# Gate matmuls that write a PSUM bank in order, and an evacuation that reads it with a stride

## The chip, the cores and the metric

One Trainium2 chip, one core of it. Times are device microseconds (us) of one execution of the whole program. Three runs of the kernel before gave 2480.03, 2481.56 and 2482.59 us; the median, 2481.56 us, is the number that the changed kernel is compared with. TensorE is written PE, VectorE DVE, ScalarE ACT, GpSimd POOL, and SyncE, which issues the transfers here, SP.

## What is computed

Two transformer blocks over 512 tokens of width 1024. The change lies in the last part, the feed-forward part of the second block (PEER): every token picks, in each of 8 heads, 16 of 128 x 128 = 16384 experts, and its output is a gated sum over them.

```
top, pos = lax.top_k(cand, PEER_TOPK)
eidx = jnp.take_along_axis(cidx, pos, axis=-1)
g = jax.nn.softmax(top, axis=-1)
u = u_tab[eidx]
v = v_tab[eidx]
a = jax.nn.gelu(jnp.einsum('thkd,td->thk', u, ht))
out = jnp.einsum('thk,thkd->td', g * a, v)
```

## The kernel before

For 384 of the 512 tokens (`ND`) the kernel does not gather expert rows. It computes all 16384 scores of a token densely, and multiplies them by a dense matrix of gates that is zero where a token did not pick an expert. (The other 128 tokens are gathered row by row, by POOL's indirect transfers, later.) An expert number is 128 * ia + ib. `peer_gates` (from L1528) builds the gates, for three tiles of 128 tokens in turn, each in four chunks of 32 tokens (`GC`), each chunk in two groups of 16 tokens (`GN`): 24 groups in all.

For a group DVE writes four tensors of 128 x 2048 fp16: `gob`, one-hot in ib (L1553); `goa`, one-hot in ia (L1554); `goh`, which is `goa` times the upper half of the gate (L1555); and `goa` again, times the lower half (L1556). Each of the three names has two buffers. For each token PE then multiplies `gob` with `goh` and with `goa`, and both products add up in PSUM (L1561): a matrix of 128 (ib, on the partitions) by 128 (ia), which is this token's gates. Four tokens share one PSUM bank of 512 fp32, so a group has 32 matmuls, each with its own weight load, and 4 banks. ACT reads each bank and writes it, scaled, to `gst` (L1563), whose layout is ib x ia x 32 tokens; after 8 banks a chunk is full and SP writes its 2 MB to HBM (L1566, tensor `gates`, 12 writes). `gst` has two buffers, the PSUM pool of `gg` six.

Between the groups the kernel also works ahead on the scores: `ahead` (called at L1565) loads 512 KB of one table (`uTr`), splits it into two fp16 halves (`uTh` on ACT, L121; `uTl` on DVE, L122), multiplies them by the tokens (`pu`, 24 matmuls of 128 x 384, L141) and applies GELU on ACT (`pa`, L1589). A scheduler sets the order on PE, DVE and ACT in this part, and each engine works through its own list in order. On PE the first product of each of a group's four banks (`goh`, 4 matmuls) stands ahead of the other 28.

Behind this part the main loop of the PEER block begins: for each of 128 ia it reads the gates back (`pg`, L1602), multiplies them with the scores on POOL (`pag`, L1605), splits the result (`pw`, L121 and L122) and multiplies it with the second table (`pacc`, L1614).

Of the kernel before, what the change touches and what calls it, by code (L numbers as in the profile page):

```python
# [14 lines left out]
AF = mybir.ActivationFunctionType  # L15
# [4 lines left out]
P = 128  # L20
# [17 lines left out]
GS = 10  # L38
# [16 lines left out]
class Block:  # L55
# [1410 lines left out]
    def pairs(self, vp, qp, val, idx, eng):  # L1466

        nc = self.nc
        eng.tensor_scalar(idx[0], idx[0], 128.0, None, op0=OP.mult)
        cand = vp.tile([P, 4, 50], F32, name="cand", tag="cand", bufs=2)  # L1470
        cidx = vp.tile([P, 4, 50], F32, name="cidx", tag="cidx", bufs=2)
        for to, dst, (a, b) in ((nc.vector, cand, val), (eng, cidx, idx)):
            off = 0
            for i, ni, j, nj in PAIRS:
                n = ni * nj
                d = dst[:, :, off:off + n].rearrange("p t (i j) -> p t i j", i=ni)
                to.tensor_tensor(d, b[:, :, None, j:j + nj].to_broadcast([P, 4, ni, nj]),
                                  a[:, :, i:i + ni, None].to_broadcast([P, 4, ni, nj]), op=OP.add)
                off += n
        return cand, cidx  # L1480
# [47 lines left out]
    def peer_gates(self, wk, e, g, gd, tt, ahead):  # L1528

        nc = self.nc  # L1530
        f = wk.tile([P, 2, P], F32, name="gab", tag="gab", bufs=1)
        nc.vector.tensor_scalar(f[:, 0], e, 1.0 / 128, -63.5 / 128, op0=OP.mult, op1=OP.add)
        nc.vector.tensor_scalar(f[:, 0], f[:, 0], 1.5 * 2.0 ** 23, -1.5 * 2.0 ** 23, op0=OP.add, op1=OP.add)
        nc.vector.scalar_tensor_tensor(f[:, 1], f[:, 0], -128.0, e, op0=OP.mult, op1=OP.add)
        ps = self.ps1("gtp")
        for j, x in enumerate((f[:, 0], f[:, 1], g)):
            nc.tensor.transpose(ps[:, P * j:P * (j + 1)], x, self.ident)

        twice = lambda x: x.unsqueeze(len(x.shape)).to_broadcast([*x.shape, 2])
        idx = wk.tile([P, 2, P, 2], F16, name="gidx", tag="gidx", bufs=2)  # L1540
        gs = wk.tile([P, 2, P, 2], F16, name="gsp", tag="gsp", bufs=2)
        nc.scalar.activation(idx, twice(ps[:, :2 * P].rearrange("p (j t) -> p j t", j=2)), AF.Copy)
        gp = twice(ps[:, 2 * P:3 * P])
        nc.scalar.activation(gs[:, 0], gp, AF.Copy, scale=2.0 ** GS)
        nc.vector.scalar_tensor_tensor(gs[:, 1], gp, 2.0 ** GS, gs[:, 0], op0=OP.mult, op1=OP.subtract)
        pairs = lambda x: x.rearrange("p t (i j) -> p t i j", j=2)
        iota = pairs(self.iota128[:, None, :]).to_broadcast([P, GN, P // 2, 2])
        for c in range(P // GC):
            stage = wk.tile([P, P, GC], F32, name="gst", tag="gst", bufs=2)
            for n in range(c * GC, c * GC + GC, GN):  # L1550
                col = lambda t: t[:, n:n + GN, None, :].to_broadcast([P, GN, P // 2, 2])
                b, a, hi = (wk.tile([P, GN, P], F16, name=f"go{x}", tag=f"go{x}", bufs=2) for x in "bah")
                nc.vector.tensor_tensor(pairs(b), iota, col(idx[:, 1]), op=OP.is_equal)  # L1553
                nc.vector.tensor_tensor(pairs(a), iota, col(idx[:, 0]), op=OP.is_equal)  # L1554
                nc.vector.tensor_tensor(pairs(hi), pairs(a), col(gs[:, 0]), op=OP.mult)  # L1555
                nc.vector.tensor_tensor(pairs(a), pairs(a), col(gs[:, 1]), op=OP.mult)  # L1556
                for q in range(0, GN, 4):
                    ps = self.ps1("gg").rearrange("p (i t) -> p i t", t=4)
                    for t in range(4):
                        for j, x in enumerate((hi, a)):  # L1560
                            nc.tensor.matmul(ps[:, :, t], b[:, q + t], x[:, q + t], start=j == 0, stop=j == 1)  # L1561
                    o = n - c * GC + q
                    nc.scalar.activation(stage[:, :, o:o + 4], ps, AF.Copy, scale=2.0 ** -GS)  # L1563
                if (n == c * GC or c % 2) and len(ahead.a) < LAG - REST:
                    ahead(early=False)  # L1565
            nc.sync.dma_start(gd[:, tt * (P // GC) + c], stage)  # L1566
# [326 lines left out]
```

## Time and profile before

| | |
|---|---|
| median of 3 runs | 2481.56 us (2480.03 to 2482.59) |
| the profiled execution, its time | 2484.21 us |
| its span, from the first to the last instruction | 2482.5 us |
| what lies around the span | 1.7 us |
| PE busy in the span | 2355.9 us (95%) |
| DVE busy | 1771.0 us (71%) |
| ACT busy | 932.2 us (38%) |
| gate matmuls, first to last start | 1419.7 to 1582.5 us |
| first matmul of the main loop's sum `pacc` | 1599.5 us |

All times in the rows below are counted from the start of the span. A matmul's duration in a row reaches from its start to the end of its way through the array, and the next one starts before that; so the pace of a run of matmuls is read from their starts, or from the pieces of the chain of waits, which give a length and a count. The granted clock is a share of 2.4 GHz: 1.00 is 2.4 GHz, 0.5 is 1.2 GHz.

### The profile page before, as it was taken

Reading aid. Unit: us, or ns where it says so; the run is one execution under the profiler, and the core shown is the slowest. Engines: PE = TensorE matmul, PEld = TensorE weight load, DVE = VectorE, ACT = ScalarE, POOL = GpSimd, SP = SyncE. Lnnn points to the kernel's source line nnn. Section 1 sums busy time; section 2 is a strip of 40 time slices with the busy share of each in tenths; the row PEclk is TensorE's granted clock in tenths of the full one; section 3 lists DMA queues with packets and bytes.
Section 4 is the critical chain, followed back from the end, with each engine's and each line's share of the span. In section 5 each row is a group of like instructions: output and inputs, shape, how many; then the busy total and the mean of one; then the engine's idle time right before and its main releaser. Section 6 shows DMA issues by size and latency. Waiting matters only on the chain.

```text
span 2482.5 us, 35960 instructions
## 1 busy us (share of the span) xinstructions
PE 2355.9 (95%) x13424; PEld 1199.5 (48%) x13424; DVE 1771.0 (71%) x3285; ACT 932.2 (38%) x1593; POOL 760.7 (31%) x757
## 2 busy tenths in 40 slices
PE   6998999989999999899899799999999999999998
PEld 3444444444443343355354477655555555555443
DVE  5998658653333332568489977688888888999896
ACT  4554543231111111365356654443333333333333
POOL 2124000000000000001157500146666666666773
PEclk9998999989999999999999999999999999999999
DMA  3411139979999998222242155659999999999895
GB/s 132 131 44 44 37 141 324 334 284 417 419 419 414 401 399 347 87 69 69 103 133 70 60 200 216 221 194 354 335 338 332 337 338 329 333 342 333 294 331 175
DMA packets 186322, 613.16 MB, mean 247 GB/s; under 512 B 17971, under 2 KB 71772, under 8 KB 159900
## 3 DMA queue, kind: packets, MB, share of 16 engines
q1 hardware_dynamic: 148988, 476.44, 52.2%
q0 software_dynamic: 36864, 134.23, 14.7%
q8 instruction: 107, 1.75, 0.3%
q14 instruction: 75, 0.61, 0.1%
q10 hardware_dynamic: 288, 0.11, 0.0%
HBM read 579.58 MB, written 27.28 MB: 244 GB/s over the span
## 4 chain that ended last, share of the span: by engine, by line
PE 62%; DVE 9%; issue 3%; ACT 3%; DMA 1%; POOL 0%; SPq 0%; DVEq 0%; ACTq 0%; POOLq 0%
PE pacc L1614 17%; PE pu L141 17%; PE w L764 9%; PE py L806 5%; PE pj L141 3%; PE gg L1561 3%; PE comb L757 2%; PE disp L731 2%; PE wout L141 2%; DMA vNr<-in_vN_dram 1%; PE pq L141 1%; DVE pef L1517 1%; DVE wlo L122 1%; DVE gacc L1771 1%; DVE t L1626 1%
## 5 line engine op out<-in xcount | busy, mean ns | idle before, releaser
L141 PE MATMUL pu<-pn,uTh 128*128 128x384 f16 x2048 | 502.8, 328 | 7.6 <-ACT pa L1589 5.7
L1614 PE MATMUL pacc<-vNh,pw 128*128 128x512 f16 x1536 | 474.2, 380 | 5.7 <-DVE pw L122 4.3
L1614 PEld LDWEIGHTS <-pw 128*128 128x128 f16 x2304 | 224.5, 98 | 275.1 <-DVE pw L122 13.1
L141 PE MATMUL pu<-pn,uTl 128*128 128x384 f16 x1024 | 335.9, 328 | 5.5 <-POOL uTl L1577 4.8
L1614 PE MATMUL pacc<-vNl,pw 128*128 128x512 f16 x768 | 292.2, 380 | 2.5 <-DVE vNl L122 2.5
L141 PEld LDWEIGHTS <-uTh 128*128 128x128 f16 x2048 | 202.1, 99 | 148.1 <-ACT uTh L121 5.8
L121 ACT ACTIVATE vNh<-vNr 128x1024 f16<-128x1024 f32 x128 | 135.2, 1056 | 315.5 <-PE pacc L1614 286.7
L764 PE MATMUL w<-wx,xt 128*64 128x512 f32 x1024 | 253.0, 597 | 0.0
L141 PEld LDWEIGHTS <-whi 128*128 128x128 f16 x1744 | 159.7, 99 | 180.9 <-issue 24.6
L1742 POOL DMA_INDIRECT row<-in_pu_dram,pe x128 | 198.7, 1552 | 125.4 <-DVE row L1764 102.5
L1742 POOL DMA_INDIRECT row<-in_pv_dram,pe x128 | 197.0, 1539 | 122.7 <-DVE gacc L1771 93.6
L122 DVE SCALAR_TENSOR_TENSOR vNl<-vNr,vNh 128x1024 f16<-128x1024 f32 x128 | 169.1, 1321 | 91.2 <-ACT vNh L121 91.1
L1142 POOL MEMSET cvu<- 128x2 f32 x4 | 0.4, 96 | 755.9 <-PE w L764 755.9
L1605 POOL TENSOR_TENSOR pag<-pa,pg 128x384 f32<-128x384 f32 x128 | 152.0, 1188 | 200.8 <-DMA pg<-gates 184.3
L122 DVE SCALAR_TENSOR_TENSOR uTl<-uTr,uTh 128x1024 f16<-128x1024 f32 x113 | 175.1, 1549 | 28.7 <-ACT uTh L121 23.2
L141 PE MATMUL pj<-wx,whi 128*128 128x512 f16 x624 | 189.3, 384 | 2.0 <-ACT wx L121 1.8
L1771 DVE SCALAR_TENSOR_TENSOR gacc<-row,ga,gacc 128x1024 f32<-128x1024 f32 x127 | 184.1, 1450 | 2.2
L1764 DVE SCALAR_TENSOR_TENSOR row<-row,htok 128x1024 f32<-128x1024 f32 x128 | 178.1, 1436 | 0.0
L122 DVE SCALAR_TENSOR_TENSOR wlo<-wraw,whi 128x1024 f16<-128x1024 f32 x97 | 130.0, 1341 | 47.7 <-ACT whi L121 47.3
L758 DVE SCALAR_TENSOR_TENSOR hT<-comb,hT 128x512 f32<-128x512 f32 x128 | 80.5, 684 | 110.9 <-PE comb L757 110.8
L1589 ACT ACTIVATE pa<-pu 128x384 f32<-128x384 f32 x128 | 62.2, 486 | 226.6 <-PE pu L141 226.5
L764 PEld LDWEIGHTS w<-wx,xt 128*64 128x64 f32 x1024 | 74.5, 137 | 141.1 <-issue 138.1
(456 smaller groups left out, 3900.3 us busy)
## 6 DMA issues: line engine op xcount, KB each, us to landing
wx<-in_w_dram SPq DMA_DIRECT2D x192, 1024.0 KB
uTr<-in_uT_dram SPq DMA_DIRECT2D x128, 512.0 KB
vNr<-in_vN_dram SPq DMA_DIRECT2D x128, 512.0 KB
wraw<-in_win_dram SPq DMA_DIRECT2D x57, 512.0 KB
wada<-in_wada_dram SPq DMA_DIRECT2D x48, 512.0 KB
gates<-gst SPq DMA_DIRECT2D x12, 2048.0 KB
pg<-gates SPq DMA_DIRECT2D x32, 768.0 KB
wraw<-in_wq_dram SPq DMA_DIRECT2D x16, 512.0 KB
```

The costliest lines, as they stand in the source:

```text
L121: self.nc.scalar.activation(hi, src, AF.Copy, scale=scale)
L122: self.nc.vector.scalar_tensor_tensor(lo, src, scale, hi, op0=OP.mult, op1=OP.subtract)
L141: self.nc.tensor.matmul(ps, w[a][:, ks[k], :], act[b][:, k, cols], start=first and k == only[0] and j == 0, stop=last and k == only[-1] an ...
L758: nc.vector.scalar_tensor_tensor(hT[:, m], ps, 2.0 ** -AS, hT[:, m], op0=OP.mult, op1=OP.add)
L764: nc.tensor.matmul(ps[64 * b:64 * b + 64], xt[q][:, 4 * c + k, 64 * b:64 * b + 64], w[b][:, k], start=c == 0 and k == 0, stop=c == 1 and k ...
L806: nc.tensor.matmul(py[d][64 * b:64 * b + 64], ht[:, f, 64 * b:64 * b + 64], w[b][:, f], start=f == 0, stop=f == 3)
L1561: nc.tensor.matmul(ps[:, :, t], b[:, q + t], x[:, q + t], start=j == 0, stop=j == 1)
L1605: nc.gpsimd.tensor_tensor(c3(ag), c3(a), self.gt[:, :, ia % 4, :], op=OP.mult)
L1614: self.nc.tensor.matmul(acc[2 * t + c], w[x][:, P * t:P * (t + 1)], v[y][:, 512 * c:512 * c + 512], start=ia == 0 and j == 0, stop=ia == P ...
L1742: nc.gpsimd.indirect_dma_start(out=t, out_offset=None, in_=I[table], in_offset=bass.IndirectOffsetOnAxis(ap=self.e[:, s:s + 1], axis=0))
L1764: nc.vector.scalar_tensor_tensor(x, x, 1.0, self.ht, op0=OP.mult, op1=OP.mult, accum_out=self.a[:, s:s + 1])
L1771: nc.vector.scalar_tensor_tensor(self.acc, x, self.a[:, s:s + 1], self.acc, op0=OP.mult, op1=OP.add)
```

## The change

The gate matmul of token t in its bank wrote its 128 fp32 results in steps of four elements (16 bytes), token innermost: PSUM held ia x 4 tokens. Now it writes 128 elements in a row, and PSUM holds 4 tokens x ia. ACT's copy, which used to read the bank from front to back, now reads for each ia four elements that are 128 elements (512 bytes) apart. What it writes is as before: for each ia a run of four tokens (16 bytes) in `gst`, the runs 128 bytes apart.

```
         for q in range(0, GN, 4):
-            ps = self.ps1("gg").rearrange("p (i t) -> p i t", t=4)
+            ps = self.ps1("gg")
             for t in range(4):
                 for j, x in enumerate((hi, a)):
-                    nc.tensor.matmul(ps[:, :, t], b[:, q + t], x[:, q + t], start=j == 0, stop=j == 1)
+                    nc.tensor.matmul(ps[:, P * t:P * (t + 1)], b[:, q + t], x[:, q + t], start=j == 0, stop=j == 1)
             o = n - c * GC + q
-            nc.scalar.activation(stage[:, :, o:o + 4], ps, AF.Copy, scale=2.0 ** -GS)
+            nc.scalar.activation(stage[:, :, o:o + 4], ps.rearrange("p (t i) -> p i t", t=4), AF.Copy, scale=2.0 ** -GS)
```

No instruction is added, removed or moved: the list of each of the five engines, and of every transfer, is the same row for row. Only the two access patterns in PSUM differ.

## Rows read from the trace of the kernel before

**Rows 1.** Busy time by stretch: us, PE, PEld, DVE, ACT, POOL busy, granted clock, DMA share, GB/s.
```profile
1440.00:1460.00 20.00, 20.00 (x155) 15.92 (x153) 16.75 (x16) 10.41 (x17) 0.00 (x0) 1.00 0.61 221
...
1419.70:1582.60 162.90, 151.80 (x1164) 121.66 (x1164) 127.91 (x118) 82.61 (x134) 0.00 (x0) 1.00 0.53 200
...
1600.00:2200.00 600.00, 600.00 (x3238) 316.32 (x3237) 526.40 (x639) 228.92 (x316) 378.01 (x283) 1.00 0.89 319
```

**Rows 2.** Waits of DVE, 1419.7 to 1582.6: us in total, times, longest.
```profile
DVE gob L1553 <- PE gg L1561: 19.4, 9, 2.4
DVE uTl L122 <- ACT uTh L121: 7.0, 1, 7.0
DVE uTl L122 <- PE pu L141: 5.5, 1, 5.5
```

**Rows 3.** Chain of waits, gate matmuls of two groups in a row: start us, us, what.
```profile
1479.56 3.52 PE gg L1561 x32
...
1484.38 3.07 PE gg L1561 x28
```

**Rows 4.** Line L1561: duration ns min/median/max, first and last start.
```profile
L1561 PE MATMUL gg<-goa,gob x384: 269/315/315, 1422.0 to 1582.6; 128*128 128x128 f16 x192
```

**Rows 5.** Line L731, the dispatch of the first block, same columns.
```profile
L731 PE MATMUL disp<-disp,ut x1024: 218/220/315, 529.4 to 984.9; 128*128 128x128 f16 x171
```

**Rows 6.** Timeline of PE in the dispatch: start us, us, engine, line, what, count.
```profile
536.38 1.96 PE L731 MATMUL disp<-disp,ut 128*128 128x128 f16 x32
```

**Rows 7.** Busy time by stretch, two stretches of the dispatch.
```profile
529.30:532.80 3.50, 3.43 (x34) 3.18 (x34) 3.33 (x6) 0.74 (x3) 0.00 (x0) 0.54 0.84 269
536.30:538.30 2.00, 2.00 (x36) 1.82 (x34) 0.35 (x1) 0.73 (x2) 0.00 (x0) 1.00 0.49 82
```

**Rows 8.** Timeline of DVE in the gates' part, six of its instructions.
```profile
1463.18 1.21 DVE L1556 TENSOR_TENSOR goa<-goa,gsp 128x2048 f16<-128x2048 f16 x1
...
1464.54 0.29 DVE L1526 TENSOR_TENSOR pgate<-pgate,pgs 128x128 f32<-128x128 f32 x1
...
1481.56 1.22 DVE L1556 TENSOR_TENSOR goa<-goa,gsp 128x2048 f16<-128x2048 f16 x1
...
1483.83 1.22 DVE L1554 TENSOR_TENSOR goa<-iota,gidx 128x2048 f16<-128x2048 f16 x1
...
1519.44 1.22 DVE L1556 TENSOR_TENSOR goa<-goa,gsp 128x2048 f16<-128x2048 f16 x1
...
1577.20 1.22 DVE L1556 TENSOR_TENSOR goa<-goa,gsp 128x2048 f16<-128x2048 f16 x1
```

**Rows 9.** Chain of waits, the last 28 matmuls of two later groups.
```profile
1522.32 3.06 PE gg L1561 x28
...
1579.86 3.06 PE gg L1561 x28
```

**Rows 10.** Timeline behind the last group: SP's write of the gates, DVE's split.
```profile
1583.58 0.33 SPq L1566 DMA_DIRECT2D gates<-gst  x1
...
1598.47 0.78 DVE L122 SCALAR_TENSOR_TENSOR pw<-pag,pw 128x384 f16<-128x384 f32 x1 [1.46 <-ACT pw L121]
```

**Rows 11.** Groups on ACT, 1419.7 to 1582.6: busy us, mean ns; idle before, releaser.
```profile
L1563 ACT ACTIVATE gst<-gg 128x512 f32<-128x512 f32 x95 | 56.7, 597 | 49.3 <-PE gg L1561 38.7 <-issue 9.9
L121 ACT ACTIVATE uTh<-uTr 128x1024 f16<-128x1024 f32 x17 | 18.0, 1057 | 32.2 <-PE pu L141 29.2 <-DVE goa L1556 1.8 <-issue 1.2
L1589 ACT ACTIVATE pa<-pu 128x384 f32<-128x384 f32 x17 | 8.1, 474 | 0.0
```

**Rows 12.** Line L106, plain copies out of PSUM on ACT: duration ns min/median/max.
```profile
L106 ACT ACTIVATE pT<-tp x16: 597/597/605, 273.6 to 341.3; 128x512 f32<-128x512 f32 x16
L106 ACT ACTIVATE wx<-htp x8: 365/383/383, 470.6 to 516.5; 128x256 f32<-128x256 f32 x8
```

**Rows 13.** Two sums of 128 elements on DVE, in steps of 8 and in order.
```profile
L839 DVE TENSOR_REDUCE ig<-selg x1: 374/374/374, 521.0 to 521.0; 128x32 f32<-128x128 f32 x1
...
L1524 DVE TENSOR_REDUCE pgs<-pgate x3: 267/279/279, 1411.6 to 1463.0; 128x8 f32<-128x128 f32 x3
```

## The prediction

> **What bounds the kernel now.** I read the busy times by stretch first, to see whether the part that builds the gates is bound by PE at all. Over its 162.9 us PE is busy 151.8 us and DVE 127.91 us, at a granted clock of 1.00, and in places PE has no free moment: 20.00 of 20 us [rows 1]. ACT is busy 82.61 us. Then DVE's waits, since DVE is the engine that would be next: it stands still 162.9 - 127.9 = 35.0 us, of which 19.4 + 7.0 + 5.5 = 31.9 us are three waits that lead to PE [rows 2]: nine times the next `gob` waits until the gate matmuls of two groups back have given its buffer free, once `uTl` waits for `pu`, and once for `uTh`, which ACT can only make after `pu`. So PE holds DVE up, and DVE then holds PE up: in the chain of waits the two take turns. Third, the pace of the gate matmuls in that chain: 32 in 3.52 us and 28 in 3.07 us [rows 3], that is 109.6 ns each. Behind this part the main loop is a matter of PE alone, 600.00 of 600 us busy [rows 1], and all its work hangs on its own start; so what the gates' part saves reaches the end of the kernel whole.
>
> **The matmuls.** 109.6 ns for 128 columns is about what PE takes at the lower of its two clocks (128 / 1.2 GHz = 107 ns), but the clock was 1.00. The dispatch of the first block shows what it should be: the same shape, fp16, 128 x 128, a new weight load for each, several products adding up in one place, and an output of 128 elements in a row. A gate matmul lasts 315 ns, a dispatch matmul 220 ns [rows 4, 5]. 32 of the dispatch take 1.96 us [rows 6]; the last one's own 0.22 us off, 31 steps of 56.1 ns. In that stretch the clock was 1.00 as well; where the dispatch begins, behind an idle PE, its clock was 0.54 [rows 7]. What gate and dispatch differ in at the same clock is the step of the output, and this is what the change takes away. So I take 56.1 ns: 53.5 ns less, 1.7 us per 32, 1.5 us per 28, and for all 768 gate matmuls 41.1 us of PE's work.
>
> Not all 41.1 us come out, since DVE is next. The bound of the gain is DVE's 35.0 us of standing still. What goes, wait by wait:
>
> (a) The nine waits of `gob`, 19.4 us. In the piece shown, the 32 matmuls from 1479.56 end 1.80 us later instead of 3.52, at 1481.36; the `pu` between take 1484.38 - 1483.08 = 1.30 us as before, to 1482.66; the next 28 need `goa`, which DVE has ready at 1481.56 + 1.22 = 1482.78 [rows 3, 8], and with 1.57 us they are done at 1484.4, some 0.2 us more for the last one's way through the array. DVE comes to the next `gob` after the `goa` that starts at 1483.83, by its 1.22 us at 1485.05 [rows 8]. The wait, up to 2.4 us before [rows 2], is gone with 0.4 us to spare. All nine: **19.4 us**.
>
> (b) `uTl` waiting 5.5 us for `pu`, at the end of the first token tile. PE comes into this from a stretch in which it was never idle [rows 1]; with 1.5 to 1.7 us less per group it catches up. What stays is the way from the last `goa`, ready at 1463.18 + 1.21 = 1464.4 [rows 8], over 28 matmuls (1.6 us) and one or two `pu` (0.3 us) to 1466.3, while DVE has nothing to do from 1464.54 + 0.29 = 1464.8 on: 1.5 us. Saved **4.0 us**.
>
> (c) `uTl` waiting 7.0 us for `uTh`, at the end of the second tile. The 28 matmuls that start at 1522.32 [rows 9] follow 32 others, so PE gets to them 1.7 us sooner, at 1520.6; `goa` is ready at 1519.44 + 1.22 = 1520.66 [rows 8]; the 28 take 1.5 us less. Saved **3.1 us**.
>
> (d) The end. The last 28 start at 1579.86 [rows 9]; PE could be there 1.7 us sooner, `goa` is ready at 1577.20 + 1.22 = 1578.42 [rows 8], so 1.4 us sooner, and they end 2.9 us sooner. But now four banks fill faster than ACT empties them: one in 7 x 56 ns = 0.4 us, against 0.597 us a copy. The last copy ends about 0.4 + 0.25 + 4 x 0.597 = 3.0 us after 1578.46, near 1581.5, and SP's write of the last gates, issued at 1583.58 before [rows 10], leaves 2.1 us sooner. The main loop's first sum hangs on both, PE's `pu` and the gates read back (`pw` ends at 1599.25 [rows 10], `pacc` starts at 1599.5), so I take the smaller: **2.1 us**.
>
> Together 19.4 + 4.0 + 3.1 + 2.1 = **28.6 us**. The profiled execution took 2484.21 us (its span and 1.7 us around it), 2.65 us more than the median; it would take 2455.6 us, and the median comes to 2481.56 - 28.6 = **2453.0 us**.
>
> **ACT's copy.** No row shows an ACT copy that reads PSUM in steps of 512 bytes. Now it takes 597 ns [rows 11], just as a copy that reads and writes in order [rows 12], though it writes runs of 16 bytes; so on the writing side the pattern costs nothing. A gain is excluded, since the copy is already as short as a plain one. For the other end I take the farthest row: DVE sums 128 elements in steps of 8 in 374 ns and in order in 279 ns [rows 13]; if all 95 ns come from the step (the first also writes four times as many results), 512 elements cost 0.38 us more, 0.98 us a copy. I take 597 ns, because of the row on ACT itself. At 0.98 us ACT needs 24 x (4 x 0.98 + (18.0 + 8.1) / 24) = 120 us [rows 11], still less than DVE's 128, and only the ends of the three tiles feel it: four copies there, 3 x 4 x 0.38 = 4.6 us, 2457.6 us.
>
> The Trainium skill speaks against the change here: SBUF — State Buffer, in the note on cachelines of its section "Door 1: The DMA port swizzle", says that an access which crosses to a new line pays a penalty, and that a line of PSUM is two fp32 values. ACT used to take two elements from each line and would take one; by that rule the copy gets dearer, by how much the page doesn't say. The writing side of row L1563, in pieces of 16 bytes at no cost, doesn't show such a penalty; no run here shows the reading side.
>
> **Rivals.** *Loads hold the pace.* If the 128 x 128 loads let PE go down only half of the way, to 83 ns, each of the nine waits in (a) shrinks by 60 x 26.7 ns = 1.6 us and keeps 0.6 of its mean 2.16 us: 14.4 us; of the other 9.2 us half goes, 4.6 us: 2481.6 - 19.0 = 2462.6 us. For it: a gate matmul has a load of its own, and nothing of the gates has run in order yet. Against it: so has a dispatch matmul. The skill's TensorE: Matmul & The Clock Gate, section "Back-to-back issue gap", gives about 81 ns for a stream of loads and matmuls of this size, which would be this rival. The dispatch here, 56.1 ns, disagrees with it.
>
> *ACT becomes the bound (slower).* ACT must do four copies and on average 26.1 / 24 = 1.09 us of other work per group. A group takes 162.9 / 24 = 6.79 us now, so from (6.79 - 1.09) / 4 = 1.4 us a copy on, ACT alone is as long as the part is now. The step from 256 to 512 elements is 214 ns [rows 12], 0.84 ns an element, over a fixed 0.17 us. At half the rate a copy takes 1.03 us, near the case above; at a quarter, 1.88 us, and the part takes 24 x (4 x 1.88 + 1.09) = 207 us: 44 us more, and some 4 us at the end, 2530 us. Against it: nothing on ACT in this trace costs more than 0.84 ns an element for its pattern.
>
> *The change does nothing for PE.* If the step in PSUM is not what makes it 109.6 ns, PE's work stays, ACT has 0.38 us a copy to spare, and the time stays at 2481.6 us.
>
> **How the numbers follow.** Forecast (56 ns, 0.6 us) 0.78, with its own range of 2446 to 2458; dearer copy below the bound 0.08, 2457.6 us; half the pace 0.05, 2462.6 us; no quicker matmuls 0.03; ACT as the bound 0.06, 2530 us. The lower end is the whole 35.0 us and the scatter of the three runs, 1.5 us: 2445; the upper takes in the dearer copy and half the pace with the same scatter, 2464; outside lie the last two, 0.09, and the tails. About 0.2%, 5 us, can be told from no change: faster 0.78 + 0.08 + 0.05 = 0.91, same 0.03, slower 0.06.
>
> **What would show it.** Gate matmuls of about 220 ns, 28 in about 1.6 us; the copy at 597 ns; no wait of `gob` for `gg`; DVE busy 128 us as now, but in a part of some 134 us, with PE at about 111 of them; a write of the gates every 134 / 12 = 11 us on the mean instead of 162.9 / 12 = 13.6; `pacc` starting near 1571 and the main loop as long as before. A copy above 0.7 us, a pace above 60 ns, or a `gob` that now waits for something else would show which step failed; a granted clock below 1.00 in the part would too, as PE now waits more.

## The result and the profile after

The changed kernel takes 2452.64 us (median of 4 runs, 2446.61 to 2457.72) against 2480.8 us for the kernel before (the three runs of the table and one more, 2479.75 to 2482.59): a ratio of 0.9885, with an interval of 0.9861 to 0.9909. Forecast were 2453.0 us. The profiled execution took 2451.42 us, its span 2449.7 us.

The gate matmuls and ACT's copy, by line (duration ns min/median/max, first and last start), where [rows 4] gave 315 ns for the matmul and [rows 11] 597 ns for the copy:

```profile
L1561 PEld LDWEIGHTS <-gob x768: 95/98/99, 1418.7 to 1553.1; 128*128 128x128 f16 x192
L1561 PE MATMUL gg<-goh,gob x384: 216/219/230, 1419.6 to 1553.1; 128*128 128x128 f16 x192
L1561 PE MATMUL gg<-goa,gob x384: 216/219/219, 1421.9 to 1553.2; 128*128 128x128 f16 x192
L1563 ACT ACTIVATE gst<-gg x96: 580/598/620, 1422.5 to 1553.7; 128x512 f32<-128x512 f32 x96
```

And in the chain of waits, where [rows 3, 9] had 3.07 and 3.06 us for 28 of them:

```profile
1551.83 1.56 PE gg L1561 x28
```

A matmul lasts 219 ns like one of the dispatch [rows 5], and 28 take 1.56 us, 55.7 ns each. The copy, which now reads in steps of 512 bytes, is 1 ns longer. The weight loads read as shorter too (98 ns, 139 ns before), without any edit to them. Busy time of the part (columns as in [rows 1]):

```profile
1419.60:1553.10 133.50, 114.56 (x1163) 81.09 (x1163) 127.05 (x118) 74.43 (x133) 0.00 (x0) 1.00 0.63 240
```

The part has gone from 162.9 to 133.5 us, 29.4 us less. PE has 37 us less to do and is no longer the fuller engine: DVE works for 127 of 133.5 us. Waits of DVE in it, in full, to be held against [rows 2]:

```profile
DVE uTl L122 <- ACT uTh L121: 4.3, 1, 4.3
DVE uTl L122 <- PE pu L141: 1.6, 1, 1.6
```

The nine waits of `gob` are gone. PE waits for DVE instead, and in the chain through this part `gg` has 2.6% where it had 50.0% before (PE's waits after, then the chain after and before):

```profile
PE gg L1561 <- DVE goa L1556: 7.2, 8, 1.9
...
PE gg L1561 <- DVE goh L1555: 4.5, 13, 0.6
```
```profile
by line: DVE goa L1554 19.4%; DVE goh L1555 19.2%; DVE gob L1553 16.3%; issue 11.3%; DVE uTl L122 10.7%; DVE goa L1556 10.0%; PE pu L141 4.4%; PE gg L1561 2.6%; ACT gst L1563 2.5%; ACT uTh L121 1.0%; ACT gidx L1542 0.7%; ACT pa L1589 0.6%; 
```
```profile
by line: PE gg L1561 50.0%; PE pu L141 18.4%; DVE gob L1553 8.1%; DVE goa L1554 7.0%; DVE goh L1555 6.3%; DVE goa L1556 5.6%; issue 1.0%; ACT uTh L121 0.8%; ACT L1589 0.8%; DVE uTl L122 0.8%; ACT pa L1589 0.6%; DVE gsp L1545 0.5%; ACT gidx 
```

What that looks like on DVE, from the timeline: each instruction starts 1.13 to 1.14 us after the one in front of it, and a `gob` that used to stand up to 2.4 us starts like any other.

```profile
1472.97 1.22 DVE L1553 TENSOR_TENSOR gob<-iota,gidx 128x2048 f16<-128x2048 f16 x1
1474.11 1.22 DVE L1554 TENSOR_TENSOR goa<-iota,gidx 128x2048 f16<-128x2048 f16 x1
1475.24 1.22 DVE L1553 TENSOR_TENSOR gob<-iota,gidx 128x2048 f16<-128x2048 f16 x1
1476.38 1.22 DVE L1555 TENSOR_TENSOR goh<-goa,gsp 128x2048 f16<-128x2048 f16 x1
```

Behind the part, the rows that answer to [rows 10], and the first sum of the main loop (timeline):

```profile
1554.34 0.33 SPq L1566 DMA_DIRECT2D gates<-gst  x1
...
1569.73 0.78 DVE L122 SCALAR_TENSOR_TENSOR pw<-pag,pw 128x384 f16<-128x384 f32 x1 [2.23 <-ACT pw L121]
...
1571.68 0.38 PE L1614 MATMUL pacc<-vNh,pw 128*128 128x512 f16 x1
```

SP's last write of the gates leaves 29.2 us sooner (1583.58 before), `pw` starts 28.7 us sooner (1598.47), `pacc` 27.8 us sooner (1599.5). So 1.6 of the 29.4 us are given back between the last gate matmul and `pacc`. They go here (busy time by stretch, PE first, the clock third from the end; the first two rows are after, the third is the same work before):

```profile
1566.40:1569.00 2.60, 2.59 (x9) 1.24 (x10) 1.09 (x1) 0.00 (x0) 0.85 (x1) 0.56 1.04 310
1569.00:1571.50 2.50, 2.50 (x13) 1.37 (x12) 1.61 (x2) 2.33 (x4) 1.09 (x2) 0.78 0.97 313
```
```profile
1595.90:1597.50 1.60, 1.56 (x10) 0.98 (x11) 1.12 (x1) 0.00 (x0) 0.61 (x1) 1.00 1.11 331
```

In both kernels PE first stands still twice on the way to the last 22 `pu`, 1.5 us for `uTh` and 0.8 us for `uTl`, and in both it was busy without a break for the 10.5 us ahead of that, at 1.00. Before, the clock stayed at 1.00 behind that pause; after, PE goes down to the lower of its levels (0.56 is close to the 0.5 of 1.2 GHz) and is back at the upper one for `pacc`. The 22 `pu` take 5.1 us (1566.41 to 1571.51) instead of 3.4 us (1595.94 to 1599.37).

From the start of `pacc` to the end of the span, 883.0 us passed before and 878.0 us after. All ten runs below lie between 877.8 and 880.2 us, with the old access pattern (878.6 and 880.0) as with the new, so the 5.0 us by which the two profiled executions differ there belong to these executions and not to the change. Ahead of the part the executions scatter as well: the first gate matmul starts between 1418.7 and 1426.0 us in the twelve profiled ones (1419.7 and 1419.6 in before and after), so medians that lie a few us apart are held against the part and not read alone.

### The profile page after: what moved, and what is told of

It is laid out like the page before. It is cut to its first block, busy times and chain, and to the rows that moved or that the text cites. A ratio compares the mean times of both kernels' runs of the same rounds, so it can differ in the third digit from the quotient of the medians.

```text
span 2449.7 us, 35960 instructions
## 1 busy us (share of the span) xinstructions
PE 2314.0 (94%) x13424; PEld 1159.5 (47%) x13424; DVE 1772.6 (72%) x3285; ACT 924.5 (38%) x1593; POOL 765.3 (31%) x757
## 4 chain that ended last, share of the span: by engine, by line
PE 59%; DVE 11%; issue 4%; ACT 3%; DMA 1%; POOL 0%; SPq 0%; DVEq 0%; ACTq 0%; POOLq 0%
PE pacc L1614 17%; PE pu L141 16%; PE w L764 9%; PE py L806 5%; PE pj L141 4%; PE comb L757 2%; PE disp L731 2%; PE wout L141 2%; DMA vNr<-in_vN_dram 1%; DVE goa L1554 1%; DVE goh L1555 1%; DVE gob L1553 1%; PE pq L141 1%; DVE pef L1517 1%; DVE uTl L122 1%
## 5 line engine op out<-in xcount | busy, mean ns | idle before, releaser
L122 DVE SCALAR_TENSOR_TENSOR vNl<-vNr,vNh 128x1024 f16<-128x1024 f32 x128 | 169.1, 1321 | 84.6 <-ACT vNh L121 84.3
```

Of the source, the lines that this page charges most:

```text
L122: self.nc.vector.scalar_tensor_tensor(lo, src, scale, hi, op0=OP.mult, op1=OP.subtract)
```

## The experiments

"The part" is the time from the first to the last start of a gate matmul; "to `pacc`" runs from the same start to the first `pacc`. The ratio of "after" is the one above; each of the others is against runs of the kernel before on the same chip (2480.07 us for runs 1 to 4, 2481.74 us for 5 to 7, 2482.53 us for 8, 9 and "after, again"; medians of 19, 17 and 7 runs). The copy of run 7 is the median over four lengths.

| run | us, median | ratio (95%) | matmul ns | copy ns | part us | to `pacc` us |
|---|---|---|---|---|---|---|
| before | | | 315 | 597 | 162.9 | 179.8 |
| after | 2452.64 | 0.9885 (0.9861 to 0.9909) | 219 | 598 | 133.5 | 152.1 |
| after, again | 2454.11 | 0.9891 (0.9873 to 0.991) | 219 | 600 | 133.5 | 152.1 |
| 1 reads with a stride | 2478.8 | 0.9994 (0.9979 to 1.0008) | 314 | 597 | 162.8 | 179.8 |
| 2 writes with a stride | 2459.94 | 0.9918 (0.9889 to 0.9948) | 219 | 1104 | 138.6 | 155.6 |
| 3 pairs | 2452.41 | 0.9898 (0.9866 to 0.993) | 219 | 598 | 133.5 | 152.0 |
| 4 steps of 8 bytes | 2481.32 | 1.0007 (0.9992 to 1.0022) | 314 | 597 | 162.9 | 179.8 |
| 5 split on POOL, after | 2471.52 | 0.9952 (0.9934 to 0.997) | 219 | 603 | 153.6 | 170.8 |
| 6 split on POOL, before | 2492.82 | 1.0045 (1.0031 to 1.0059) | 314 | 597 | 174.7 | 189.5 |
| 7 copies up to four times as long | 2489.25 | 1.0032 (1.0021 to 1.0043) | 219 | 1877 | 160.7 | 184.2 |
| 8 half of L1556, after | 2445.61 | 0.9853 (0.9826 to 0.9881) | 219 | 597 | 123.4 | 142.3 |
| 9 half of L1556, before | 2468.34 | 0.9947 (0.9928 to 0.9965) | 314 | 597 | 149.9 | 169.1 |

**1. Only the reading changed.** From the kernel before; the matmuls keep their steps of 16 bytes.

```
-ps = self.ps1("gg").rearrange("p (i t) -> p i t", t=4)
+ps = self.ps1("gg")
-nc.tensor.matmul(ps[:, :, t], ...)
+nc.tensor.matmul(ps.rearrange("p (i t) -> p i t", t=4)[:, :, t], ...)
-nc.scalar.activation(stage[:, :, o:o + 4], ps, AF.Copy, ...)
+nc.scalar.activation(stage[:, :, o:o + 4], ps.rearrange("p (t i) -> p i t", t=4), AF.Copy, ...)
```

> ACT's half of the change alone: the gate matmuls write in steps of 16 bytes as in the kernel before, and ACT reads the bank in steps of 512 bytes as in the changed one. The gates of the four tokens of a bank are mixed up by that; nothing is left out. Theory (the step of PE's output sets its pace, reading costs ACT nothing): gate matmuls 315 ns and 28 in 3.06 us, the copy 597 ns, the time that of the kernel before, 2481 us, within 3 us. Rival 1 (the gain came from ACT's new reading, which frees banks sooner): the time of the changed kernel, about 2453 us. Rival 2 (reading in steps costs ACT something that the changed kernel hides): copies over 0.65 us, or a time some us above 2481.

Lines L1561 and L1563, and DVE's first wait, in this run:

```profile
L1561 PE MATMUL gg<-goa,gob x384: 269/314/314, 1425.4 to 1586.0; 128*128 128x128 f16 x192
...
L1563 ACT ACTIVATE gst<-gg x96: 579/597/599, 1426.4 to 1586.4; 128x512 f32<-128x512 f32 x96
```
```profile
DVE gob L1553 <- PE gg L1561: 19.4, 9, 2.4
```

The copy costs what it cost, the matmuls too, and the wait is 19.4 us to the digit. The whole gain comes from the writing side. The Trainium skill's rule that the prediction weighed against the change (SBUF — State Buffer, the note on cachelines in "Door 1: The DMA port swizzle") states the penalty for a new line of SBUF, and of PSUM's lines it speaks for matmuls; carried over to ACT's read, as the prediction did, it would have this read pay at each element. The 597 ns disagree with that.

**2. ACT reads in order and writes with a stride.** From the changed kernel: the matmuls in order, the copy in the order of PSUM, so that it writes 512 single fp32, neighbours 128 bytes apart.

```
-nc.scalar.activation(stage[:, :, o:o + 4], ps.rearrange("p (t i) -> p i t", t=4), AF.Copy, ...)
+nc.scalar.activation(stage[:, :, o:o + 4].rearrange("p i t -> p t i"), ps.rearrange("p (t i) -> p t i", t=4), AF.Copy, ...)
```

> PE's half alone: matmuls write in order, ACT reads the bank in order too, and writes 128 elements in steps of 128 bytes four times over instead of runs of four tokens. Theory: the pattern costs ACT nothing on either side, so copy 597 ns, gate matmuls 219 ns, and the time of the changed kernel, 2453 us within 5. Rival (a pattern in steps costs ACT in SBUF, since now no two neighbours are written together): copies of 0.8 us or more, and 2455 to 2465 us.

Line L1563, the part, the wait that is new on PE, and DVE's two longest waits:

```profile
L1563 ACT ACTIVATE gst<-gg x96: 1042/1104/1188, 1427.9 to 1565.2; 128x512 f32<-128x512 f32 x96
```
```profile
1425.00:1563.60 138.60, 116.16 (x1165) 82.86 (x1165) 127.41 (x118) 111.59 (x133) 0.00 (x0) 0.99 0.62 233
```
```profile
PE gg L1561 <- ACT gst L1563: 6.0, 9, 0.7
```
```profile
DVE uTl L122 <- ACT uTh L121: 5.6, 1, 5.6
DVE gob L1553 <- ACT gidx L1542: 1.7, 1, 1.7
```

The expectation that a stride costs ACT nothing on either side fell: in single values the write takes 507 ns more, 0.99 ns an element. It also is a run of the prediction's rival of the dearer copy. That one put 4.6 us on a copy of 0.98 us, felt at the ends of the three tiles alone; at 1.10 us its arithmetic gives 3 x 4 x 0.51 = 6.1 us. The part is 5.1 us longer than after. DVE's waits show where: 1.3 us more for `uTh` at the end of the second tile and 1.7 us for `gidx` (made on ACT, behind the copies) at the end of the first, which was not there before; and from the last `goa` (1559.46) to the last gate matmul (1563.55) 4.1 us pass, where after took 2.8 (1550.38 to 1553.17). That is 4.3 us at the ends of the three tiles, where the rival had put them; the nine waits of PE for `gst` come on top without holding DVE up. So the rival's mechanism was sound, and the order of the copy's output is the half of the edit that has to be kept. The median is 7.5 us above that of run 3 on the same chip, but the profiled execution of run 2 also began the part 6.3 us later than that of run 3, so the 5.1 us of the part are the better measure.

**3 and 4. How much order is enough.** From the changed kernel, the layout of a bank. In run 3 each matmul writes pairs of neighbours (8 bytes), 32 bytes from pair to pair. In run 4 it writes single values in steps of 8 bytes. ACT's copy is turned to fit.

```
-nc.tensor.matmul(ps[:, P * t:P * (t + 1)], b[:, q + t], x[:, q + t], ...)
+nc.tensor.matmul(ps.rearrange("p (i t j) -> p i t j", t=4, j=2)[:, :, t], b[:, q + t], x[:, q + t].rearrange("p (i j) -> p i j", j=2), ...)    (run 3)
+nc.tensor.matmul(ps.rearrange("p (h i t) -> p h i t", h=2, t=2)[:, t // 2, :, t % 2], b[:, q + t], x[:, q + t], ...)    (run 4)
```

> Matmuls write pairs of neighbouring elements (8 bytes), the pairs 32 bytes apart; ACT reads them back in the order of the gates. Theory A (PE writes two neighbouring fp32 at a time, and a step breaks this up): pairs are as good as a full row: gate matmuls 219 ns, 28 in 1.55 us, 2453 us within 5. Theory B (any jump in PSUM costs, a pair then at least half of it): 28 matmuls in 2.3 to 3.1 us, and 2460 to 2481 us.

> Matmuls write every second element (steps of 8 bytes, two tokens interleaved). Theory A (two neighbours at a time): as slow as steps of 16 bytes: gate matmuls 315 ns, 28 in 3.06 us, 2481 us within 3. Theory B (the cost grows with the step): between the two, 28 matmuls in 2 to 2.5 us and 2455 to 2470 us.

Line L1561 of run 3, then of run 4:

```profile
L1561 PE MATMUL gg<-goh,gob x384: 216/219/230, 1418.7 to 1552.2; 128*128 128x128 f16 x192
```
```profile
L1561 PE MATMUL gg<-goh,gob x384: 269/314/314, 1422.5 to 1585.2; 128*128 128x128 f16 x192
```

Pairs run at full pace, and a step of 8 bytes is as slow as one of 16. What a matmul pays for is thus, of the steps tried, not the size but that no two neighbouring values are written next to each other. The Trainium skill (PSUM — Partial Sum Buffer, "Specifications (TRN2)") gives lines of 8 bytes, which fits both runs; its remark there that any pattern that is not contiguous slows matmuls does not fit run 3.

**5 and 6. Less work for DVE.** If DVE sets the pace after, taking its `uTl` away should shorten the part after by much and the part before by little. An existing option does that: POOL makes `uTl` (L1577). The same edit on both kernels:

```
-                    ahead(early=False)
+                    ahead(early=True)
```

> On the changed kernel, the split of the scores' table in the gates' part (uTl, 18 times some 1.14 us of DVE) goes to POOL, which is idle there, with one more copy on ACT for each, as the kernel does it already in the part before. Theory (DVE sets the pace of the part now): DVE's work falls from 127 to 107 us, PE has 768 x 56 ns + 408 x 163 ns = 110 us, ACT 92 us; the part shortens from 133 to 115 to 120 us, the time to 2435 to 2440 us. Rival (something else sets the pace, ACT or the order of the lists): the part stays over 128 us and the time within 5 us of 2453.

> The same move of uTl to POOL on the kernel before, where the gate matmuls take 109 ns each. Theory (PE and DVE took turns there, PE with 768 x 109 ns + 408 x 163 ns = 150 us of work): the part can't fall below 150 us from 163, so the time to 2470 to 2478 us, a smaller gain than the same move brings on the changed kernel. Rival (DVE was the bound before as well): as much as on the changed kernel, 2460 to 2466 us.

Both missed: the changed kernel lost some 17 to 19 us by it, the kernel before 11 us. Groups of run 5 by line, then a piece of its timeline:

```profile
L1577 POOL TENSOR_TENSOR uTl<-uTr,uTh 128x1024 f16<-128x1024 f32 x15 | 42.5, 2832 | 87.2 <-ACT uTr L1576 87.2
```
```profile
L1555 DVE TENSOR_TENSOR goh<-goa,gsp 128x2048 f16<-128x2048 f16 x23 | 37.6, 1634 | 0.0
L1554 DVE TENSOR_TENSOR goa<-iota,gidx 128x2048 f16<-128x2048 f16 x23 | 37.4, 1626 | 0.0
```
```profile
1474.04 2.12 POOL L1577 TENSOR_TENSOR uTl<-uTr,uTh 128x1024 f16<-128x1024 f32 x1 [6.56 <-ACT uTr L1576]
1474.20 3.05 DVE L1554 TENSOR_TENSOR goa<-iota,gidx 128x2048 f16<-128x2048 f16 x1
...
1477.17 1.21 DVE L1553 TENSOR_TENSOR gob<-iota,gidx 128x2048 f16<-128x2048 f16 x1
1477.51 2.85 POOL L1577 TENSOR_TENSOR uTl<-uTr,uTh 128x1024 f16<-128x1024 f32 x1 [1.34 <-ACT uTr L1576]
1478.30 3.14 DVE L1555 TENSOR_TENSOR goh<-goa,gsp 128x2048 f16<-128x2048 f16 x1
1481.36 1.21 DVE L1554 TENSOR_TENSOR goa<-iota,gidx 128x2048 f16<-128x2048 f16 x1
```

The two engines take turns here. POOL starts 0.16 us ahead of `goa`, and `goa` ends 1.09 us after POOL is done (1476.16), about the 1.14 us from one start to the next that DVE needs undisturbed. POOL's next one starts inside a `gob` and lasts 0.73 us longer than its 2.12 us, about what `gob` still had to run; the `goh` behind it then ends 1.08 us after POOL. Fifteen `uTl` took 15 x 1.22 = 18.2 us off DVE, and DVE's busy time still rose from 127.05 to 136.64 us: 27.8 us came on, 1.85 us for each of POOL's. The Trainium skill (SBUF — State Buffer, "SBUF: two separate sides") describes just that, a pair of ports that a GpSimd operation and a DVE operation with two SBUF inputs hold in turn, each for its whole length; the timeline agrees. By these rows each `uTl` can hold DVE up for as long as POOL's 2.12 us and frees it of 1.22 us, so the run could have been expected to lose. The scheduler also put the lists in another order in both runs, and new waits came on (7.1 us of `gob` for `gidx`, 5.6 us of `gab` for `gtp` in run 5). PE, which now waits longer (13.7 us for `goh` in run 5, up to 3.2 us at a time), did not keep its clock in the part either: 0.93 in run 5, 0.98 in run 6. So these runs tell nothing about who sets the pace.

**7. ACT as the bound.** From the changed kernel; each copy writes its four tokens up to four times over (as far as `gst` reaches, and later copies write the right ones on top), so that ACT has more to do and the other engines have the same work.

```
-nc.scalar.activation(stage[:, :, o:o + 4], ps.rearrange("p (t i) -> p i t", t=4), AF.Copy, ...)
+k = min(4, (GC - o) // 4)
+nc.scalar.activation(stage[:, :, o:o + 4 * k].rearrange("p i (r t) -> p i r t", t=4), ps.rearrange("p (t i) -> p i t", t=4)[:, :, None, :].to_broadcast([P, P, k, 4]), AF.Copy, ...)
```

> On the changed kernel, each copy of ACT reads its bank up to four times over and writes the repeats where the later copies of the same chunk write afterwards: 2048 elements instead of 512 in five of eight copies, then 1536, 1024 and 512. The gates are the same. Theory (a copy takes 0.17 us and 0.84 ns an element): 1.88 us for the long ones and 1.56 on the mean, ACT needs 24 x (4 x 1.56 + 1.09) = 176 us, more than the 163 us of the part before; ACT is the bound, and the time some 15 to 20 us above the kernel before, 2495 to 2500 us. Rival (ACT's work still lies beside PE's and DVE's): under 2480 us.

ACT's groups by shape and the busy times, both from the first gate matmul to the end of the last copy, and PE's first wait:

```profile
L1563 ACT ACTIVATE gst<-gg 128x2048 f32<-128x2048 f32 x60 | 116.5, 1944 | 2.0 <-PE gg L1561 1.5 <-DMA gates<-gst 0.2
L121 ACT ACTIVATE uTh<-uTr 128x1024 f16<-128x1024 f32 x19 | 21.6, 1136 | 1.2 <-issue 1.2
L1563 ACT ACTIVATE gst<-gg 128x1536 f32<-128x1536 f32 x12 | 18.5, 1538 | 0.0
L1563 ACT ACTIVATE gst<-gg 128x1024 f32<-128x1024 f32 x12 | 13.3, 1111 | 0.0
L1589 ACT ACTIVATE pa<-pu 128x384 f32<-128x384 f32 x20 | 11.2, 560 | 1.1 <-PE pu L141 1.1
L1563 ACT ACTIVATE gst<-gg 128x512 f32<-128x512 f32 x12 | 8.3, 690 | 0.0
```
```profile
1419.30:1590.80 171.50, 133.85 (x1228) 92.03 (x1227) 130.57 (x119) 168.31 (x140) 0.00 (x0) 0.94 0.53 195
```
```profile
PE gg L1561 <- ACT gst L1563: 15.3, 17, 1.9
```

With copies of 1.63 us on the mean (156.6 us by 96) the gain is gone, and the kernel is slower than before by its interval, 7.5 us; that lies between the 2495 to 2500 us of the theory and the 2480 us of its rival. This is the prediction's rival of ACT as the bound, with its sign, and the rows show where it acts: ACT is busy for 168.31 of 171.5 us, and PE waits for `gst`. (The scheduler chose another order of the lists here too, and the clock was 0.94; neither was separated from the copies.) It was costed too high: by its formula ACT would need 24 x (4 x 1.63 + 1.09) = 183 us, and it is through in 171.5, with more of its other work in the stretch than the formula had. The reason is in these rows: the durations add up to 156.6 + 21.6 + 11.2 = 189.4 us and some smaller ones, but ACT was busy for 168.31 us, because each instruction starts before the one in front of it has ended. An ACT copy's duration is not its pace.

**8 and 9. DVE's work made less without POOL.** The second product with the gate (L1556) is done for 8 of a group's 16 tokens.

```
-nc.vector.tensor_tensor(pairs(a), pairs(a), col(gs[:, 1]), op=OP.mult)
+nc.vector.tensor_tensor(pairs(a)[:, :GN // 2], pairs(a)[:, :GN // 2], col(gs[:, 1])[:, :GN // 2], op=OP.mult)
```

> On the changed kernel, DVE multiplies only the first 8 of a group's 16 tokens by the lower half of the gate (L1556, 128 x 1024 instead of 128 x 2048); for the other 8 tokens the product of the gate's lower half is left out, and the one-hot matrix stands in its place. All matmuls stay. Theory (DVE sets the pace of the part now): 24 x 0.53 = 12.8 us less work of DVE, of which 9 to 12 us come out: 2441 to 2444 us. Rival (PE or the order of the lists sets the pace): within 4 us of the changed kernel's 2453.

> The same halved product on the kernel before, with the same lists in the same order as the run on the changed kernel. Theory (PE's 109 ns matmuls hold DVE up there, and DVE waits anyway): less than half of the 12.8 us come out, 3 to 6 us: 2475 to 2478 us. Rival (DVE set the pace there as much as now): 9 to 12 us, 2469 to 2472 us.

The changed kernel against itself, 2454.11 to 2445.61 us, gained 8.5 us of the 24 x (1.22 - 0.68) = 13 us that were taken off DVE. The part of run 8:

```profile
1423.30:1546.70 123.40, 114.00 (x1161) 81.54 (x1161) 114.30 (x118) 74.73 (x133) 0.00 (x0) 0.99 0.69 259
```

DVE's 127 us have become 114, the part follows (10.1 us), and now PE and DVE are even. That is what DVE as the pace after would give. But the kernel before gained no less: 14.2 us by the medians (8.7 to 17.9 us by the interval), where 3 to 6 were expected and the rival said 9 to 12. Up to `pacc` the two gains are 9.8 us in run 8 and 10.7 us in run 9, hardly apart. So the pair of runs does not show that DVE is the bound after and was not before. The part, DVE's waits and PE's waits in run 9, and PE's waits in the kernel before:

```profile
1419.30:1569.20 149.90, 148.13 (x1161) 121.66 (x1161) 115.61 (x118) 80.74 (x134) 0.00 (x0) 1.00 0.57 215
```
```profile
DVE gob L1553 <- PE gg L1561: 14.0, 13, 1.8
DVE uTl L122 <- ACT uTh L121: 13.3, 5, 6.6
```
```profile
PE gg L1561 <- DVE goh L1555: 1.2, 3, 0.6
PE pu L141 <- DVE uTl L122: 1.2, 2, 0.6
```
```profile
PE pu L141 <- ACT pa L1589: 5.7, 7, 1.3
PE gg L1561 <- DVE goa L1556: 4.6, 8, 1.7
PE gg L1561 <- DVE goh L1555: 1.3, 3, 0.6
```

PE is busy 148.13 of 149.9 us: here it is the bound with hardly a gap. In the kernel before, PE had 11 us of gaps in the part (162.9 - 151.8), and nine of them are gone. In these two runs the scheduler also chose another order of the lists than in the kernels they come from (the same one in both). It likely has a share in this: half of PE's gaps before were waits of `pu` for ACT's `pa`, which the halved product does not shorten, and they went too. How much of the 14.2 us belongs to that order was not separated and stays open, and so does its share in the 8.5 us.

**The change once more**, with no edit, on the chip of runs 8 and 9.

> The changed kernel once more, beside the others on one chip. Theory: 2453 us within 4, gates' part 133 us, and the scatter of single runs, some 10 us, comes from the end of the main loop, where PE waits for the second table and its clock falls, and not from the gates' part. Rival (the change has made the gates' part uneven): a gates' part some us away from 133.

It gave 0.9891, with its interval in the table, the same part of 133.5 us, and the same two waits of DVE, 4.3 and 1.6 us; so the gates' part does not scatter. Where the scatter lies came out only in part as expected: this profiled execution took 4.6 us more than the first one of the changed kernel, 3.1 of them ahead of the first gate matmul (1422.7 for 1419.6) and 1.5 behind the start of `pacc`. The lower clock ahead of `pacc` is there again, 0.57 in the first 2.6 us of the 22 `pu`, and in run 3 as well, 0.57. It also shows in runs 8 (0.54) and 9 (0.59), where the matmuls of run 9 write in steps as before; in run 2 it does not show (1.00), though its matmuls write in order, nor in runs 1, 4, 5, 6 and 7 (1.00).

## Why the prediction was right, step by step

- **The pace.** 56.1 ns were taken from the dispatch; 55.7 ns came out (28 in 1.56 us). The inference from one line to another, same shape, same clock, other step, held, and runs 1, 3 and 4 show that the step was the cause. The rival by which loads hold the pace at 83 ns, and with it the Trainium skill's figure of about 81 ns for such a stream (TensorE: Matmul & The Clock Gate, "Back-to-back issue gap"), is refuted by the same row.
- **(a)** All 19.4 us of `gob`'s waits are gone, and run 1, where they are all there, shows that ACT's new reading has no share in that.
- **(b)** 1.5 us were to remain of `uTl` waiting for `pu`; 1.6 us did. **(c)** 3.9 us were to remain of the wait for `uTh`; 4.3 us did. So 3.9 and 2.7 us went, for 4.0 and 3.1.
- **(d)** This term was mis-sized twice, in opposite directions. SP's write leaves 29.2 us sooner, and (a) to (c) brought 19.4 + 3.9 + 2.7 = 26.0 us of that, so the end brought 3.2 us there for 2.1 forecast. Some 0.3 us of the difference is the price in "four banks fill faster than ACT empties them", 0.597 us for each of the last copies. They do fill faster, but four copies take 2.06 us together, (2.06 - 0.60) / 3 = 0.49 us from start to start. Another 0.6 us is that the last 28 matmuls come 28.0 us sooner in the chain (1551.83 for 1579.86 [rows 9]), 2.0 us beyond (a) to (c) for 1.4 forecast. A wait that goes takes a little more than itself with it: behind a wait the DVE instruction in front has run its full 1.22 us, without one the next starts after 1.14 us. By our estimate that is 9 x 0.08 = 0.7 us for the nine waits, and DVE's busy time fell by 0.86 us (127.91 to 127.05) with the same 118 instructions.

```profile
1552.25 2.06 ACT L1563 ACTIVATE gst<-gg 128x512 f32<-128x512 f32 x4 [1.31 <-PE gg L1561]
```

 On the other side, the way from there to `pacc` was taken to be as long as before, and it was longer: `pw` is ready at 1569.73 + 0.78 = 1570.5, but PE comes to it only at 1571.5, after `pu` at the lower clock. At the clock of before, the 22 `pu` would have ended at 1566.41 + 3.43 = 1569.8, and `pacc` would have started behind `pw`, near 1570.7: about 1 us of the net result is the clock's. The prediction named a clock below 1.00 as a way to be wrong, but in the gates' part, where it did not fall.
- **The copy.** 597 ns were taken, 598 ns came out. The bound that was set aside, 0.98 us, turned up on the other side of the copy, in run 2: that the pattern costs nothing in writing held for the runs of 16 bytes of [rows 11], and those could not show what single values cost.
- **The sum.** `pacc` starts 27.8 us sooner (forecast 28.6, "near 1571", measured 1571.7), and the medians differ by 2480.8 - 2452.64 = 28.2 us, or 2482.53 - 2454.11 = 28.4 us in the second comparison. The larger difference of the two profiled executions, 32.8 us, has 5.0 us from the main loop that are scatter. That the forecast lies within 0.4 us of the median is luck in part: the misses of the steps, -0.1 us in (b), -0.4 in (c), +1.1 up to SP's write and -1.4 from there to `pacc`, cancel in part, and single runs of the changed kernel lie 11 us apart. That the saving reaches the end whole was read from 600 us of a main loop of 880 us; the loop's length in the ten runs bears it out.
- **What would show it.** DVE 127.05 us in 133.5 (128 in 134 forecast) and PE 114.56 us (111; its busy time counts each matmul's way through the array, which shows wherever a run of matmuls ends). No `gob` wait came back in another form. SP's 12 writes run from 1428.0 to 1554.3, one every 11.5 us (133.5 / 12 = 11.1 us by the forecast's way of counting, for 11).

That DVE is what limits the part after was predicted from its waits and is borne out by the chain, where DVE's lines have three quarters of the part; run 8 fits it but does not show it alone. It was no safe guide to what the next edit would do: taking work off DVE by way of POOL made both kernels slower.

## What to carry to other kernels

Compare a run of matmuls that is slow at full clock with another line of the same shape in the same trace, and look at the step of its output first: two neighbouring fp32 in PSUM were enough for full pace, single values at both steps tried cost twice as much. Let the engine that evacuates PSUM (ACT here) take over the stride on its reading side, and keep its writes in runs; then bound the gain by the idle time of the engine that is next, wait by wait, and not by the matmul time saved (29.4 of 41.1 us here, with 35.0 us of idle time). Price a queue of copies by the distance of their starts and not by their durations, and before moving work from DVE to POOL look for rows in which the two run side by side.

## What was not expected of the hardware

- A matmul's write in steps of 8 bytes is as slow as in steps of 16 (314 ns and 109 ns from one to the next, 28 in 3.07 us), and pairs of 8 bytes, 32 bytes apart, are as fast as a full row (219 ns).
- For ACT the two sides differ: reading PSUM in steps of 512 bytes is free (598 ns), and so is writing runs of 16 bytes; writing single fp32 at steps of 128 bytes nearly doubles the copy (1104 ns).
- DVE's fp16 operations on two tensors and POOL's subtraction held each other out, in the rows shown for whole instructions: 1.22 us became 3.05 and 3.14 us beside POOL, and 2.12 us of POOL became 2.85 us beside DVE.
- Behind the same short pause (1.5 and 0.8 us idle) PE went on at 1.00 in some runs (before, 1, 2, 4, 5, 6 and 7) and at 0.54 to 0.59 in others (after, its repetition, runs 3, 8 and 9), and that cost 1.7 us of `pu` in the changed kernel. What decides between the two was not found.
